# A hybrid decoder layer on one core: projections, S5 scan and attention heads in one written order, and the third modulation moved to the merge

## The chip, the core and the metric

The kernel runs on one core of a Trainium2 chip. The metric is the device time of one execution, in microseconds, as the median of several runs. The engines that matter are TensorE (PE, with its weight loads PEld), VectorE (DVE), ScalarE (ACT), GpSimd (POOL) and the DMA queue of SyncE (SPq). Each of them takes its own instructions in the order in which the program lists them, and waits where an input or a buffer isn't ready.

## The reference

One decoder layer for one sequence of 512 tokens and 2048 channels, in float32. A conditioning vector gives six modulations of 2048 values. The normed input is projected to queries, keys and values (8 heads of 128), a forget gate, an S5 input of 512 channels and two gates of 2048. S5 is a complex scan along the tokens (2048 states); the heads are causal softmax attention with a bias from the summed forget gate. Both results go through an up-projection, are weighed by their gates, added and projected by `w_out`. A feed-forward with 16384 retrieved experts follows.

```python
mod = cond @ w_ada[l] + b_ada[l]
sh1, sc1, g1, sh2, sc2, g2 = jnp.split(mod, N_MOD, axis=-1)
h = modulate(rms_norm(x, norm1_w[l]), sh1, sc1)
proj = h @ w_in[l]
q, k, v, f_logit, u, gate_s, gate_a = jnp.split(proj, IN_SPLIT_POINTS, axis=-1)
y_ssm = half_glu(s5_mixer(u, ...), w_glu[l], b_glu[l])
y_attn = fox_attention(q, k, v, f_logit, b_forget[l], q_norm_w[l], k_norm_w[l])
merged = (jax.nn.sigmoid(gate_s) * (y_ssm @ w_ssm_up[l])
          + jax.nn.sigmoid(gate_a) * (y_attn @ w_attn_up[l]))
x = x + g1[:, None, :] * (merged @ w_out[l])
...
```

## The kernel before

All weights are float32 and are multiplied in three passes: each is split into a rounded part `whi` and a rest `wlo`, and three matmuls (`L82` to `L84`, or `L147` to `L149`) make one product. A unit of weights is four blocks of 128 rows by 256 columns, 512 KB: `wload` fetches it into `wf`, ACT casts it to `whi` (`L88`), DVE subtracts to get `wlo` (`L89`), and 48 matmuls of 256 columns or 24 of 512 use it. `whi` and `wlo` have two buffers each.

The stages follow each other. **Start** computes the first two modulations, the normed input `h` and the S5 input `u`, and prepares S5's constants; the tables of cosines and sines (`ctab`, `stab`) are built on POOL there. **Projections** come next: the forget gate, then for each pair of heads `hp` the queries, keys and values (`proj_tok`, four units each), and at the end the first gates. `qk` norms queries or keys: raw copies out of PSUM (`L743`), eight squares with sums on DVE (`L748`), a root on ACT (`L190`), small steps on DVE (`L191` to `L195`), a multiplication (`L753`), eight transposes on PE (`L759`). S5 and the heads run beside the projections: `tick()` is called after each unit and lets the generators in `self.bg` take steps, S5 half a step and the heads one. An S5 step is a quarter of a 128-channel block: two products `bu` on PE, multiplications and scans on DVE, six multiplications and sums on POOL (`L692` to `L698`), and products into `y` on PE (`L700`, `L701`). A head's step scores one block of 128 tokens and transposes and multiplies the earlier ones (`L790` to `L815`). The third modulation, `ada(2, ...)`, is worked on there too: 64 tiles `adaw` of 256 KB, each multiplied into a sum on DVE (`L247`).

A scheduler sets the order within this stage: it puts instructions where their inputs are due, and the loads and splits of weights stand first (`high_priority(4000)`). Only the start and the experts are in written order (`manual_schedule`).

**Half GLU and merge** follow: eight rounds `jp`, each one unit of S5's up-projection, two of the heads', and eight of the next gates. `ada` for the last three modulations runs beside them, 12 calls of 16 tiles `y` of 256 KB. These take their buffers from the pool `yp` with 28 buffers, of which 24 hold the heads' and S5's results. Then come `w_out`, the routes to the experts, and the experts themselves.

Of the kernel before, what the change touches and what calls it, by code (L numbers as in the profile page):

```python
# [17 lines left out]
P = 128  # L18
S = 512
# [19 lines left out]
TODO = ('tg', '', 'tgw', '', 'tg', '', 'tg', 'm')  # L39
PE_ROWS = (2, 3, 5, 6, 7, 12)  # L40
# [17 lines left out]
class Builder:  # L58
# [77 lines left out]
    def proj_tok(self, w2d, nk, c0, act, pool, tag):  # L136

        mm = self.nc.tensor.matmul
        ps = [self.t(pool, [P, 2, 256], F32, tag) for _ in range(2)]
        for k0 in range(0, nk, 4):  # L140
            hi, lo = self.wunit(w2d, k0, 4, c0, 256)
            for t in range(TT):
                o = ps[t // 2][:, t % 2, :]
                for k in range(4):
                    kk = k0 + k
                    ah, al = (x[:, t * P:(t + 1) * P] for x in act(kk))
                    mm(o, ah, hi[:, k, :], start=kk == 0 and t % 2 == 0, stop=False, skip_group_check=True)  # L147
                    mm(o, ah, lo[:, k, :], start=False, stop=False, skip_group_check=True)
                    mm(o, al, hi[:, k, :], start=False, stop=kk == nk - 1, skip_group_check=True)  # L149
            self.tick()  # L150
        return ps
# [105 lines left out]
    def start(self, es, w_u):  # L257


        nc, V, G = self.nc, self.nc.vector, self.nc.gpsimd  # L260
# [19 lines left out]
        def load():  # L280

            while seq and (free or seq[0][0] == "x"):
# [18 lines left out]
                tiles[key] = t, slot  # L301

# [40 lines left out]
        def rest(q, accs, rows):  # L343
# [8 lines left out]
            ws = []  # L352
            for c in range(2):
                wf = take("w", q, c)
# [4 lines left out]
                load()  # L359
# [11 lines left out]
            late = None  # L371
            for k in range(q * 4, q * 4 + 4):
# [97 lines left out]
    def s5_setup(self, loads):  # L470
# [24 lines left out]
        cs, sn = nt("s5c0"), nt("s5s0")  # L495
# [22 lines left out]
        for l in range(7):  # L518
            c2, s2, tq = (self.t(cp if l == 6 else self.s5w, [P, J], F32, f"s5p{l}{x}") for x in "cst")
# [11 lines left out]

        ct = self.ct = self.t(self.tabp, [P, J, P], F32, "ctab")
        st = self.st = self.t(self.tabp, [P, J, P], F32, "stab")
        nc.gpsimd.memset(ct[:, :, 0:1], 1.0)
        nc.gpsimd.memset(st[:, :, 0:1], 0.0)
        n = 1
        for l in range(7):
            cb = pc[l][:, :, None].to_broadcast([P, J, n])
            sb = pn[l][:, :, None].to_broadcast([P, J, n])
            tm = self.t(self.s5w, [P, J, n], F32, "tabt")  # L540
            lo, hi = slice(0, n), slice(n, 2 * n)
# [74 lines left out]
    def s5_mats(self, m):  # L616
        nc, sp = self.nc, self.s5p
        bt = []
        for i in range(2):
            ps = self.t(self.ptp, [P, P], F32, "tp")  # L620
            nc.tensor.transpose(ps, self.pb[i][:, 4 * m:4 * m + 4].rearrange("p j a c -> p (j a c)"), self.ident)
            b = self.t(sp, [P, 4, P], F32, "bt", bufs=2)
            nc.gpsimd.memset(b, 0.0)
            for jj in range(4):
                r = slice(32 * jj, 32 * jj + 32)
                nc.scalar.copy(b[r, jj, :], ps[r, :])
            bt.append(b)
        ctm = []
        for i in range(2):
            ps = self.t(self.ptp, [P, P], F32, "tp")  # L630
            nc.tensor.transpose(ps, self.cd[i][:, m].rearrange("p a s -> p (a s)"), self.ident)
            c = self.t(sp, [P, 640], F32, "cm", bufs=2)
            nc.gpsimd.memset(c, 0.0)
            for g in range(2):
                r = slice(64 * g, 64 * g + 64)
                dst = c.rearrange("p (j r) -> p j r", r=160)[r, :, 16 * g:16 * g + 16]
                src = ps.rearrange("p (j r) -> p j r", r=32)[r, :, 16 * g:16 * g + 16]
                nc.scalar.activation(dst, src, AF.Copy, scale=1.0 if i == 0 else -1.0)
            ctm.append(c)
        return bt, ctm  # L640

    def s5_tile(self, m, jj, bt, u):
        nc, sp = self.nc, self.s5p
        j = 4 * m + jj
        br = self.t(self.ps5, [P, S], F32, "bu", bufs=2)
        nc.tensor.matmul(br, bt[0][:, jj, :], u, start=True, stop=True)
        bi = self.t(self.ps5, [P, S], F32, "bu", bufs=2)
        nc.tensor.matmul(bi, bt[1][:, jj, :], u, start=True, stop=True)
        c4 = self.ct[:, j, None, :].to_broadcast([P, 4, P])
        s4 = self.st[:, j, None, :].to_broadcast([P, 4, P])  # L650

        def v(x):
# [4 lines left out]
        wi = self.t(sp, [P, S], F32, "w", bufs=4)
        tm = self.t(sp, [P, S], F32, "tmv")
        V.tensor_mul(v(tm), v(bi), s4)
        V.tensor_mul(v(wr), v(br), c4)  # L660
        V.tensor_add(wr, wr, tm)
        tm = self.t(sp, [P, S], F32, "tmv")
        V.tensor_mul(v(tm), v(br), s4)
        V.tensor_mul(v(wi), v(bi), c4)
        V.tensor_sub(wi, wi, tm)
        mg = self.mag[:, j:j + 1].to_broadcast([P, P])
        rc, rs = self.rot[0][:, j:j + 1], self.rot[1][:, j:j + 1]
        ini = (0.0, 0.0)
        for c in range(4):
            sl = slice(c * P, (c + 1) * P)  # L670
            V.tensor_tensor_scan(wr[:, sl], mg, wr[:, sl], ini[0], op0=ALU.mult, op1=ALU.add)
            V.tensor_tensor_scan(wi[:, sl], mg, wi[:, sl], ini[1], op0=ALU.mult, op1=ALU.add)
            if c < 3:
                q = self.t(sp, [P, 4], F32, "car", bufs=4)
                e = slice(c * P + P - 1, c * P + P)
                V.tensor_mul(q[:, 0:1], wi[:, e], rs)
                V.tensor_mul(q[:, 1:2], wr[:, e], rs)
                V.scalar_tensor_tensor(q[:, 2:3], wr[:, e], rc, q[:, 0:1], op0=ALU.mult, op1=ALU.subtract)
                V.scalar_tensor_tensor(q[:, 3:4], wi[:, e], rc, q[:, 1:2], op0=ALU.mult, op1=ALU.add)
                ini = (q[:, 2:3], q[:, 3:4])  # L680
        return wr, wi, c4, s4

    def s5_out(self, jj, wr, wi, c4, s4, ctm, yps):
        nc, sp, G = self.nc, self.s5p, self.nc.gpsimd

        def v(x):
            return x.rearrange("p (c t) -> p c t", c=4)

        sr = self.t(sp, [P, S], F32, "s", bufs=2)
        si = self.t(sp, [P, S], F32, "s", bufs=2)  # L690
        tp = self.t(sp, [P, S], F32, "tmg")
        G.tensor_mul(v(tp), v(wi), s4)  # L692
        G.tensor_mul(v(sr), v(wr), c4)
        G.tensor_sub(sr, sr, tp)
        tp = self.t(sp, [P, S], F32, "tmg")
        G.tensor_mul(v(tp), v(wr), s4)
        G.tensor_mul(v(si), v(wi), c4)
        G.tensor_add(si, si, tp)  # L698
        cs = slice(jj * P, (jj + 1) * P)
        nc.tensor.matmul(yps, ctm[0][:, cs], sr, start=jj == 0, stop=False)  # L700
        nc.tensor.matmul(yps, ctm[1][:, cs], si, start=False, stop=jj == 3)  # L701

    def s5(self, m):
        nc = self.nc
        bt, ctm = self.s5_mats(m)
        yps = self.t(self.ps5, [P, S], F32, "y", bufs=1)
        u = self.u[m]
        z = None
        for jj in range(5):
            zn = self.s5_tile(m, jj, bt, u) if jj < 4 else None  # L710
            if z:
                self.s5_out(jj - 1, *z, ctm, yps)
            z = zn
            yield
        nc.vector.scalar_tensor_tensor(u, u, self.col2[:, 6 + m:7 + m], yps, op0=ALU.mult, op1=ALU.add)


    def forget(self, fps):
        nc, ap = self.nc, self.attp
        z = self.t(ap, [NH, S], F32, "fz")  # L720
# [1139 lines left out]
```

## Time and profile before

| | us |
|---|---|
| median of 3 runs | 3833.74 |
| lowest and highest | 3831.94, 3837.95 |
| the profiled execution, its time | 3826.62 |
| its span in the trace | 3824.6 |
| start, 0 to 173.8 | 173.8 |
| projections, S5, heads, half GLU, 173.8 to 744.1 | 570.3 |
| merge, 744.1 to 1209 | 464.9 |
| `w_out`, 1209 to 1396 | 187.0 |
| routes, 1396 to 1710 | 314.0 |
| experts, 1710 to the end | 2114 |

The limits of the stages are read from the trace, where the first or last instruction of a stage stands. The profiled execution is 7.1 us shorter than the median, and 2.0 us of its time lie outside its span. PE is busy for 3640.0 us of the span. A busy PE isn't always a PE at full speed: its granted clock is shown in each window, and matmuls overlap each other.

### The profile page before, as it was taken

Reading aid. Unit: us, or ns where it says so; the run is one execution under the profiler, and the core shown is the slowest. Engines: PE = TensorE matmul, PEld = TensorE weight load, DVE = VectorE, ACT = ScalarE, POOL = GpSimd, SP = SyncE. Lnnn points to the kernel's source line nnn. Section 1 sums busy time; section 2 is a strip of 40 time slices with the busy share of each in tenths; the row PEclk is TensorE's granted clock in tenths of the full one; section 3 lists DMA queues with packets and bytes.
Section 4 is the critical chain, followed back from the end, with each engine's and each line's share of the span. In section 5 each row is a group of like instructions: output and inputs, shape, how many; then the busy total and the mean of one; then the engine's idle time right before and its main releaser. Section 6 shows DMA issues by size and latency. Waiting matters only on the chain.

```text
span 3824.6 us, 58662 instructions
## 1 busy us (share of the span) xinstructions
PE 3640.0 (95%) x22966; PEld 3346.6 (88%) x22966; DVE 3027.7 (79%) x4704; ACT 1287.6 (34%) x2140; POOL 928.9 (24%) x680
## 2 busy tenths in 40 slices
PE   5988889999999999999989999999999999999998
PEld 2576768778887879899989999999999999999997
DVE  7678776555555358967879999999999988999997
ACT  2323323522222242245643333333333333333332
POOL 4142331000000024523411222222222212222221
PEclk8999989999999999999999999999999999999999
DMA  7723223366665542238889999999999979999996
GB/s 272 253 67 94 78 74 115 116 204 209 193 194 160 142 117 82 93 114 305 299 315 305 347 369 372 369 354 372 370 369 368 367 282 324 374 371 352 370 369 217
DMA packets 467081, 967.39 MB, mean 253 GB/s; under 512 B 66378, under 2 KB 335860, under 8 KB 400116
## 3 DMA queue, kind: packets, MB, share of 16 engines
q1 hardware_dynamic: 411508, 560.97, 44.9%
q0 software_dynamic: 55296, 402.68, 27.2%
q8 instruction: 180, 2.95, 0.3%
q14 instruction: 97, 0.79, 0.1%
HBM read 926.51 MB, written 36.96 MB: 252 GB/s over the span
## 4 chain that ended last, share of the span: by engine, by line
PE 78%; DVE 13%; DMA 4%; POOL 2%; issue 2%; ACT 1%; SPq 0%; DVEq 0%; ACTq 0%; POOLq 0%
PE A L84 8%; PE A L82 8%; PE A L83 8%; PE V L83 7%; PE V L84 7%; PE V L82 7%; PE tp L1426 6%; PE mm L82 4%; PE mm L84 4%; PE mm L83 4%; PE mx L82 2%; PE mx L83 2%; PE mx L84 2%; PE W L1262 2%; DMA y<-in_w_ada_dram 1%
## 5 line engine op out<-in xcount | busy, mean ns | idle before, releaser
L82 PE MATMUL V<-ghi,vhi 128*128 128x320 f32 x2048 | 651.8, 318 | 7.1 <-ACT vhi L1406 6.7
L82 PE MATMUL A<-hi,uhi 128*128 128x320 f32 x2048 | 657.6, 321 | 0.0
L84 PE MATMUL V<-ghi,vlo 128*128 128x320 f32 x2048 | 633.9, 310 | 3.9 <-DVE vlo L1409 3.9
L83 PE MATMUL V<-glo,vhi 128*128 128x320 f32 x2048 | 634.0, 310 | 1.6 <-DVE glo L1487 1.5
L84 PE MATMUL A<-hi,ulo 128*128 128x320 f32 x2048 | 633.0, 309 | 0.0
L83 PE MATMUL A<-lo,uhi 128*128 128x320 f32 x2048 | 632.6, 309 | 0.0
L1430 ACT CAST uhi<-tp 128x512 fp32r<-128x512 f32 x512 | 301.1, 588 | 609.5 <-PE tp L1426 608.3
L1336 DVE SCALAR_TENSOR_TENSOR big<-g,av,big 128x2048 f32<-128x2048 f32 x190 | 445.5, 2345 | 9.7 <-DMA g<-in_peer_v_dram,ids 7.2
L1324 DVE SCALAR_TENSOR_TENSOR g<-g,big 128x2048 f32<-128x2048 f32 x192 | 438.4, 2284 | 16.9 <-DMA g<-in_peer_u_dram,ids 8.0
L88 ACT CAST whi<-wf 128x1024 fp32r<-128x1024 f32 (+1 forms) x209 | 217.5, 1041 | 692.8 <-PE mx L83 223.9
L89 DVE TENSOR_TENSOR wlo<-wf,whi 128x1024 fp32r<-128x1024 f32 (+1 forms) x174 | 228.6, 1314 | 213.0 <-ACT whi L88 185.8
L82 PEld LDWEIGHTS V<-ghi,vhi 128*128 128x128 f32 x2048 | 385.9, 188 | 9.4 <-ACT vhi L1406 6.9
L84 PEld LDWEIGHTS V<-ghi,vlo 128*128 128x128 f32 x2048 | 385.3, 188 | 4.3 <-DVE vlo L1409 4.3
L83 PEld LDWEIGHTS V<-glo,vhi 128*128 128x128 f32 x2048 | 386.3, 189 | 2.7 <-DVE glo L1487 2.6
L83 PEld LDWEIGHTS A<-lo,uhi 128*128 128x128 f32 x2048 | 386.0, 188 | 0.0
L82 PEld LDWEIGHTS A<-hi,uhi 128*128 128x128 f32 x2048 | 385.7, 188 | 0.0
L84 PEld LDWEIGHTS A<-hi,ulo 128*128 128x128 f32 x2048 | 384.7, 188 | 0.0
L1437 DVE TENSOR_TENSOR ulo<-tp,uhi 128x512 fp32r<-128x512 f32 x428 | 291.1, 680 | 52.1 <-ACT uhi L1430 42.7
L1409 DVE TENSOR_TENSOR vlo<-vf,vhi 128x1024 fp32r<-128x1024 f32 x248 | 302.4, 1220 | 31.6 <-ACT vhi L1406 31.5
L1406 ACT CAST vhi<-vf 128x1024 fp32r<-128x1024 f32 x248 | 259.5, 1047 | 167.4 <-PE V L83 130.4
L1426 PE MATMUL tp<-ident,uf 128*128 128x128 f32 x2048 | 306.5, 272 | 0.3 <-DVE ulo L1437 0.3
L247 DVE SCALAR_TENSOR_TENSOR y<-y,cond,y 128x512 f32<-128x512 f32 x180 | 141.8, 788 | 172.8 <-DMA y<-in_w_ada_dram 171.4
(471 smaller groups left out, 7505.1 us busy)
## 6 DMA issues: line engine op xcount, KB each, us to landing
uf<-in_peer_u_dram SPq DMA_DIRECT2D x128, 1024.0 KB
vf<-in_peer_v_dram SPq DMA_DIRECT2D x248, 512.0 KB
wf<-in_w_in_dram SPq DMA_DIRECT2D x115, 512.0 KB
y<-in_w_ada_dram SPq DMA_DIRECT2D x192, 256.0 KB
wd<-ev SPq DMA_DIRECT2D x40, 512.0 KB
wt<-wd SPq DMA_DIRECT2D x128, 160.0 KB
adaw<-in_w_ada_dram SPq DMA_DIRECT2D x32, 512.0 KB
wf<-in_w_ada_dram SPq DMA_DIRECT2D x32, 512.0 KB
```

The source lines that it names most:

```text
L82: mm(ps, lhi, rhi, start=start, stop=False)
L83: mm(ps, lhi, rlo, start=False, stop=False)
L84: mm(ps, llo, rhi, start=False, stop=stop)
L88: nc.scalar.copy(hi, src)
L89: return (lo_eng or nc.vector).tensor_sub(lo, src, hi.bitcast(F32))
L1324: V.scalar_tensor_tensor(g, g, 1.0, hr, op0=ALU.mult, op1=ALU.mult, accum_out=av[:, s:s + 1])
L1336: V.scalar_tensor_tensor(acc, g, av[:, s:s + 1], acc, op0=ALU.mult, op1=ALU.add)
L1406: nc.scalar.copy(vhi, vf)
L1409: V.tensor_sub(vlo, vf, vhi.bitcast(F32))
L1426: mm(tp[:, k], ufs[i][:, (4 * c + k) * P:(4 * c + k + 1) * P], self.ident, is_transpose=True, start=k == 0, stop=False, skip_group_check=True)
L1430: nc.scalar.copy(hi, tp)
L1437: late.append(on_pe if i < ND0 - 3 else lambda: V.tensor_sub(lo, tp, hi.bitcast(F32)))
```

## The change

The forget gate, the queries, keys and values, and the first gates now take their units from one list, `stream(units)`, and stand with S5 and the heads in one `manual_schedule()`: what the program says is the order of every engine there. A unit is worked on in quarters of 12 matmuls (in the gates, too). After its first quarter the next unit's `whi` is cast; `tick()` follows each quarter; after the first `tick()` the next unit's `wlo` is made.

S5 is one generator with about ten steps for each of its 16 blocks. It builds its tables itself, on DVE (48 instructions), and its last six operations are on DVE as well. The squares in `qk` are on ACT. `qk` is a generator of 11 steps, and a head has 14, in the order "s0", "r0 s1", "r1 s2", "t0" and so on. The rates of steps for each `tick()` are 1.0 for `qk` and the forget gate, 0.66 for heads (1.0 during the first gates), and 2.0 for S5 until the first queries are done, 0.92 afterwards. `tick()` itself is as it was: it adds the rate to `b[2]` at each call, whether the list `b[0]` has a generator in it or not.

The lower parts of the weight splits in the start go from POOL to DVE. `ada(2, ...)` leaves the projections; the merge has two calls in each round, 16 calls and 256 tiles in all. The gates of round 1 stand ahead of the merge of round 0.

```diff
+RT = 2.0
+R5 = 0.92
+RH = 0.66
+RL = 1.0
...
+    def uhi(self, i):
+        if i < len(self.units):
+            cols = self.units[i][3]
+            hi, lo = (self.t(self.wpool, [P, 4, cols], F32R, x, bufs=2) for x in ("whi", "wlo"))
+            self.nc.scalar.copy(hi, self.uf[i])
+            self.us[i] = hi, lo
+
+    def ulo(self, i):
+        if i < len(self.units):
+            hi, lo = self.us[i]
+            self.nc.vector.tensor_sub(lo, self.uf.pop(i), hi.bitcast(F32))
+            self.uload()
+
+    def unit(self, parts):
...
+        hi, lo = self.us.pop(i)
+        for n, part in enumerate(parts):
+            part(hi, lo)
+            if n == 0:
+                self.uhi(i + 1)
+            self.tick()
+            if n == 0:
+                self.ulo(i + 1)
...
-                self.split(hi, lo, wf, G)
+                nc.scalar.copy(hi, wf)
...
+            for c, sub in enumerate(subs):
+                V.tensor_sub(*sub)
+                take("w", q, c)
+                load()
...
-            nc.gpsimd.tensor_mul(tm, st[:, :, lo], sb)
-            nc.gpsimd.tensor_mul(ct[:, :, hi], ct[:, :, lo], cb)
-            nc.gpsimd.tensor_sub(ct[:, :, hi], ct[:, :, hi], tm)
...
+    def s5(self):
+        nc, sp, V = self.nc, self.s5p, self.nc.vector
+        yield from self.s5_tables()
+        bt = [self.t(sp, [P, 4, P], F32, f"bt{i}") for i in range(2)]
+        cm = [self.t(sp, [P, 640], F32, f"cm{i}") for i in range(2)]
+        for x in bt + cm:
+            V.memset(x, 0.0)
+        yield
...
-        G.tensor_mul(v(tp), v(wi), s4)
-        G.tensor_mul(v(sr), v(wr), c4)
-        G.tensor_sub(sr, sr, tp)
...
+            V.tensor_mul(v(tm), v(wi), s4)
+            V.tensor_mul(v(sr), v(wr), c4)
+            yield
+            V.tensor_sub(sr, sr, tm)
...
-                    nc.vector.scalar_tensor_tensor(j, x[:, t, h], 1.0, x[:, t, h], op0=ALU.mult, op1=ALU.mult,
-                                                   accum_out=ms[:, 2 * b + t, h:h + 1])
+                    nc.scalar.activation(j, raw[b][:, t, h], AF.Square, accum_out=ms[:, 2 * b + t, h:h + 1])
...
-        for i in range(TT + 2):
-            if i < TT:
-                score(i)
-            if 0 <= i - 1 < TT:
-                trans(i - 1)
-            if 0 <= i - 2 < TT:
-                value(i - 2)
+        for step in ("s0", "r0 s1", "r1 s2", "t0", "r2 s3", "t1", "r3 v0", "t2", "v1", "t3", "v2", "v3"):
+            for x in step.split():
+                {"s": score, "r": scale, "t": trans, "v": value}[x[0]](int(x[1]))
             yield
...
+            bs5 = [[self.s5()], RT, 0.0]
+            bpo = [[], 1.0, 0.0]
+            bat = [[], RH, 0.0]
+            self.bg = [bpo, bat, bs5]
+            bpo[0].append(self.forget(self.mproj(1)[0]))
+            for hp in range(4):
+                qs, ks = [], []
+                bpo[0].append(self.qk(self.raw(self.mproj_tok()), self.col2[:, 0:1], qs))
+                bs5[1] = R5
+                bpo[0].append(self.qk(self.raw(self.mproj_tok()), self.col2[:, 1:2], ks))
+                v = self.v_tok(self.mproj_tok())
+                self.flush(bpo)
+                self.flush(bat)
+                bat[0].extend(self.head(hp * 2 + i, qs, ks, v) for i in range(2))
+            bat[1] = RL
+            sg = self.gates(0, self.apool, "a")
...
-            self.ada(2, hp, self.adap, 2)
...
+        sgs = [sg, self.gates(1, self.apool, "a")]
         for jp in range(8):
-            self.merge(jp, sg, ys, yh)
-            if jp < 7:
-                sg = self.gates(jp + 1, self.sgp, "sg")
-            for n in range(3 * jp // 2, 3 * (jp + 1) // 2):
-                self.ada(3 + n % 3, n // 3, self.yp, tag="y")
+            self.merge(jp, sgs.pop(0), ys, yh)
+            if 0 < jp < 7:
+                sgs.append(self.gates(jp + 1, self.sgp, "sg"))
+            for n in range(2 * jp, 2 * jp + 2):
+                self.ada(2 + n % 4, n // 4, self.yp, tag="y")
```

How the order of instructions moves is shown at three places. The names are tiles with the number that the program gives them; `x2` is two instructions of that form.

The first is on PE, around the transposes of a normed tile (`t`) in the first pair of heads. Before, they stand in the key phase (`mm_1719` and `mm_1720` are its accumulators):

```order
L149 MATMUL mm_1719<-whi_1777,h_821 128x256
L147 MATMUL mm_1720<-whi_1777,h_774 128x256
L148 MATMUL mm_1720<-wlo_1778,h_774 128x256
L759 MATMUL tp_1705<-ident_64,t_1676 128x128 x2
L759 MATMUL tp_1712<-ident_64,t_1676 128x128 x2
L149 MATMUL mm_1720<-whi_1777,h_775 128x256
...
L149 MATMUL mm_1720<-whi_1777,h_821 128x256
L759 MATMUL tp_1705<-ident_64,t_1686 128x128 x2
L759 MATMUL tp_1712<-ident_64,t_1686 128x128 x2
L147 MATMUL mm_1720<-whi_1777,h_774 128x256
```

After, in the phase that follows the one whose tile is normed (`mm_1705` is its accumulator):

```order
L201 MATMUL mm_1705<-whi_1616,h_547 128x256
L202 MATMUL mm_1705<-wlo_1617,h_547 128x256
L203 MATMUL mm_1705<-whi_1616,h_548 128x256
L867 MATMUL tp_1750<-ident_64,t_1701 128x128 x2
L867 MATMUL tp_1750<-ident_64,t_1703 128x128 x2
L867 MATMUL tp_1757<-ident_64,t_1701 128x128 x2
L867 MATMUL tp_1757<-ident_64,t_1703 128x128 x2
L201 MATMUL mm_1705<-whi_1616,h_501 128x256
```

What moved: the two halves `t` stood apart, with 11 projection matmuls between them; now all eight transposes stand together, behind the first 12 matmuls of the phase, and so they do for all eight normed tiles.

The second is on PE at the beginning of the first pair of heads. Before (`L779` is the head's bias, `L790` a score):

```order
L149 MATMUL mm_2438<-whi_2441,h_608 128x256
L779 MATMUL tp_2493<-fz_1325,PT_2494 128x512
L790 MATMUL tp_2501<-a_2072,a_1710 128x128
L147 MATMUL mm_2437<-whi_2671,h_774 128x256
L148 MATMUL mm_2437<-wlo_2672,h_774 128x256
...
L148 MATMUL mm_2437<-wlo_2672,h_789 128x256
L790 MATMUL tp_2511<-a_2072,a_1710 128x256
L149 MATMUL mm_2437<-whi_2671,h_790 128x256
```

After (`L889` the bias, `L901` scores, `L920` transposes, `L929` products with the values):

```order
L203 MATMUL mm_2398<-whi_2318,h_548 128x256
L889 MATMUL tp_2417<-fz_1337,oh_2415 128x512
L901 MATMUL tp_2423<-a_2094,a_1755 128x128
L901 MATMUL tp_2433<-a_2094,a_1755 128x256
L901 MATMUL tp_2443<-a_2094,a_1755 128x384
L920 MATMUL tp_2450<-ident_64,S_2425 128x128
L901 MATMUL tp_2457<-a_2094,a_1755 128x512
...
L929 MATMUL tp_2496<-PT_2489,a_2394 128x128 x2
L929 MATMUL tp_2496<-PT_2489,a_2396 128x128 x2
L889 MATMUL tp_2505<-fz_1337,oh_2503 128x512
L901 MATMUL tp_2511<-a_2101,a_1762 128x128
```

What moved: the head's matmuls stood between projection matmuls; now the whole head stands in one piece, and the second head of the pair (`tp_2505`) follows it in the same piece. There are four such pieces, one for each pair.

The third is on DVE in the merge. Before, between the `wlo` of successive units stand the sums of the modulations (`y`):

```order
L89 TENSOR_TENSOR wlo_7236<-wf_7233,whi_7235 128x1024
L247 SCALAR_TENSOR_TENSOR y_7412<-y_7455,cond_93,y_7412 128x512
L247 SCALAR_TENSOR_TENSOR y_7412<-y_7458,cond_93,y_7412 128x512
L89 TENSOR_TENSOR wlo_7266<-wf_7263,whi_7265 128x1024
L245 TENSOR_SCALAR y_7821<-y_7822,cond_93 128x512
L247 SCALAR_TENSOR_TENSOR y_7821<-y_7825,cond_93,y_7821 128x512
L89 TENSOR_TENSOR wlo_7296<-wf_7293,whi_7295 128x1024
L247 SCALAR_TENSOR_TENSOR y_7821<-y_7828,cond_93,y_7821 128x512
L89 TENSOR_TENSOR wlo_7326<-wf_7323,whi_7325 128x1024
```

After:

```order
L95 TENSOR_TENSOR wlo_6955<-wf_6952,whi_6954 128x1024
L301 SCALAR_TENSOR_TENSOR y_7172<-y_7197,cond_93,y_7172 128x512
L301 SCALAR_TENSOR_TENSOR y_7172<-y_7200,cond_93,y_7172 128x512
L301 SCALAR_TENSOR_TENSOR y_7172<-y_7203,cond_93,y_7172 128x512
L301 SCALAR_TENSOR_TENSOR y_7172<-y_7206,cond_93,y_7172 128x512
L95 TENSOR_TENSOR wlo_6985<-wf_6982,whi_6984 128x1024
L301 SCALAR_TENSOR_TENSOR y_7172<-y_7209,cond_93,y_7172 128x512
L301 SCALAR_TENSOR_TENSOR y_7172<-y_7212,cond_93,y_7172 128x512
L301 SCALAR_TENSOR_TENSOR y_7172<-y_7215,cond_93,y_7172 128x512
L95 TENSOR_TENSOR wlo_7015<-wf_7012,whi_7014 128x1024
```

What moved: where two or fewer sums stood between two `wlo`, there are now three or four.

## Rows read from the trace of the kernel before

**Rows 1.** Stage windows: us; then busy (count) PE, PEld, DVE, ACT, POOL; PEclk, DMA.

```profile
173.80:744.10 570.30, 499.46 (x3155) 424.99 (x3156) 396.79 (x891) 201.62 (x374) 152.23 (x108) 0.93 0.30 91
744.10:1209.00 464.90, 460.10 (x2015) 370.79 (x2014) 270.59 (x332) 110.60 (x127) 24.83 (x15) 1.00 0.65 199
```

**Rows 2.** Waits of 173.8 to 744.1: us in total, times, longest.

```profile
PE tp L759 <- DVE t L753: 29.8, 9, 7.0
...
PE tp L805 <- ACT S L798: 18.8, 8, 5.0
...
PE y L701 <- POOL s L698: 12.0, 5, 2.6
...
PE y L700 <- POOL s L694: 5.8, 3, 2.6
```

**Rows 3.** Timeline: start, duration; two successive projection matmuls of 256 columns, two of 512.

```profile
263.05 0.28 PE L148 MATMUL mm<-wlo,h 128*128 128x256 f32 x1
...
263.17 0.28 PE L149 MATMUL mm<-whi,h 128*128 128x256 f32 x1
...
685.03 0.39 PE L83 MATMUL mm<-h,whi 128*128 128x512 f32 x1
...
685.26 0.40 PE L84 MATMUL mm<-h,wlo 128*128 128x512 f32 x1
```

**Rows 4.** Timeline from 229.8: the end of a query norm beside POOL.

```profile
229.84 0.17 DVE L191 RECIPROCAL ms<-ms 128x8 f32<-128x8 f32 x1
...
230.97 1.29 POOL L693 TENSOR_TENSOR s<-w,ctab 128x512 f32<-128x512 f32 x1
...
231.06 1.22 DVE L193 TENSOR_TENSOR ms<-ms,ms 128x8 f32<-128x8 f32 x1
...
234.82 0.69 DVE L753 TENSOR_TENSOR t<-t,ms 128x512 f32<-128x512 f32 x1
```

**Rows 5.** Groups of 173.8 to 744.1: busy us, mean ns, idle before.

```profile
L89 DVE TENSOR_TENSOR wlo<-wf,whi 128x1024 fp32r<-128x1024 f32 x59 | 87.0, 1475 | 96.8 <-ACT whi L88 96.3 <-DMA adaw<-in_w_ada_dram 0.4
L88 ACT CAST whi<-wf 128x1024 fp32r<-128x1024 f32 x59 | 61.7, 1047 | 171.0 <-PE mm L149 122.7 <-issue 16.8 <-DVE car L677 16.5
...
L743 ACT COPY t<-mm 128x512 f32<-128x512 f32 x16 | 9.2, 577 | 8.9 <-PE mm L149 8.9
L190 ACT ACT_TABLE_LOAD x7 | 9.0, 1283 | 0.1
...
L665 DVE TENSOR_TENSOR w<-w,tmv 128x512 f32<-128x512 f32 x16 | 10.7, 667 | 0.0
```

**Rows 6.** Timeline of one head, 680.17 to 697.43.

```profile
680.17 1.12 PE L779 MATMUL tp<-fz,PT 8*128 8x512 f32 x2
...
684.00 0.40 ACT L796 ACTIVATE S<-S,sm 128x128 f32<-128x128 f32 x1 [0.78 <-DVE sm L795]
...
684.40 0.49 ACT L796 ACTIVATE S<-S,sm 128x256 f32<-128x256 f32 x1
...
693.85 0.72 ACT L798 ACTIVATE S<-S,sm 128x512 f32<-128x512 f32 x1 [0.23 <-DVE sm L797]
...
696.03 1.09 PE L814 MATMUL tp<-PT,a 128*128 128x128 f32 x8
...
697.16 0.27 ACT L815 COPY yo<-tp 128x128 f32<-128x128 f32 x1 [0.90 <-PE tp L814]
```

**Rows 7.** Merge: groups of DVE, busy us, mean ns, idle before.

```profile
L247 DVE SCALAR_TENSOR_TENSOR y<-y,cond,y 128x512 f32<-128x512 f32 x180 | 141.8, 788 | 172.8 <-DMA y<-in_w_ada_dram 171.4
L89 DVE TENSOR_TENSOR wlo<-wf,whi 128x1024 fp32r<-128x1024 f32 x80 | 100.8, 1260 | 6.5 <-ACT whi L88 6.2
```

**Rows 8.** Windows of 20 us in the merge, line L247 alone: DVE busy (count), PEclk, DMA.

```profile
760.00:780.00 20.00, 8.99 (x11) 1.00 0.71 226
...
980.00:1000.00 20.00, 3.76 (x5) 1.00 0.55 156
800.00:820.00 20.00, 6.76 (x9) 1.00 0.74 225
```

More of the change, by code (lines that the diff above doesn't have):

```diff
@@ L145, in proj_tok @@
                     kk = k0 + k
-                    ah, al = (x[:, t * P:(t + 1) * P] for x in act(kk))
+                    ah, al = (x[:, t * P:(t + 1) * P] for x in self.h[kk])
                     mm(o, ah, hi[:, k, :], start=kk == 0 and t % 2 == 0, stop=False, skip_group_check=True)
                     mm(o, ah, lo[:, k, :], start=False, stop=False, skip_group_check=True)
-                    mm(o, al, hi[:, k, :], start=False, stop=kk == nk - 1, skip_group_check=True)
-            self.tick()
+                    mm(o, al, hi[:, k, :], start=False, stop=kk == KT - 1, skip_group_check=True)
+            self.unit([lambda hi, lo, t=t: part(hi, lo, t) for t in range(TT)])
         return ps
@@ L301, in load @@
                 tiles[key] = t, slot
+            if not seq:
+                for slot in list(free):
+                    if slot[0] is self.wpool:
+                        free.remove(slot)
+                        self.uload()
         def take(*key):
@@ L614, in s5_setup @@
             self.cd.append(c)
[L616 to L640, printed above, removed]
@@ L657, in s5_tile @@
[L657 to L668, printed above, removed]
@@ L669, in s5_tile @@
[L669 to L680, printed above, removed]
@@ L703, in s5, with inputs @@
[L703 to L713, printed above, removed]
-            yield
-        nc.vector.scalar_tensor_tensor(u, u, self.col2[:, 6 + m:7 + m], yps, op0=ALU.mult, op1=ALU.add)
+        def inputs(m):
+            tps = []
+            for i in range(2):
+                ps = self.t(self.ptp, [P, P], F32, "tp")
+                nc.tensor.transpose(ps, self.pb[i][:, 4 * m:4 * m + 4].rearrange("p j a c -> p (j a c)"), self.ident)
+                for jj in range(4):
+                    r = slice(32 * jj, 32 * jj + 32)
+                    nc.scalar.copy(bt[i][r, jj, :], ps[r, :])
@@ new lines, in first, with last @@
+        def first(j):
+            m, jj = divmod(j, 4)
+            b = bus[j] = [self.t(self.ps5, [P, S], F32, "bu", bufs=2) for _ in range(2)]
+            for i in range(2):
+                nc.tensor.matmul(b[i], bt[i][:, jj, :], self.u[m], start=True, stop=True)
+        def last(j):
+            m, jj = divmod(j, 4)
+            if jj == 0:
+                self.yps = self.t(self.ps5, [P, S], F32, "y", bufs=1)
+            sr, si = ys.pop(j)
+            cs = slice(jj * P, (jj + 1) * P)
+            nc.tensor.matmul(self.yps, cm[0][:, cs], sr, start=jj == 0, stop=False)
+            nc.tensor.matmul(self.yps, cm[1][:, cs], si, start=False, stop=jj == 3)
@@ L718, in forget @@
+        last(NJ - 1)
+        yield
+        yield
+        end(3)
     def forget(self, fps):
         nc, ap = self.nc, self.attp
-        z = self.t(ap, [NH, S], F32, "fz")
+        z = self.cum = self.t(ap, [NH, S], F32, "fz")
         nc.vector.tensor_scalar(z, fps[0:NH, :], self.bf, None, op0=ALU.add)
@@ L725, in forget @@
         nc.scalar.activation(e, e, AF.Ln, bias=1.0)
+        for _ in range(6):
+            yield
         nc.vector.scalar_tensor_tensor(z, z, 0.0, e, op0=ALU.min, op1=ALU.subtract)
@@ L728, in forget @@
                                      op0=ALU.mult, op1=ALU.add)
-        self.cum = z
+        for _ in range(4):
+            yield
         ps = self.t(self.ptp, [P, TT, NH], F32, "tp")
@@ L1739, in build @@
         self.wa = a["w_ada"][0].rearrange("(p i) n -> p i n", i=KT)
-        with ExitStack() as r0, tc.manual_schedule():
-            self.start(r0, w[:, 3080:3592])
+        units = [(w, k, 3072, P) for k in range(0, KT, 4)]
+        for c in [x * 1024 + hp * 256 for hp in range(4) for x in range(3)] + list(GB):
+            units += [(w, k, c, 256) for k in range(0, KT, 4)]
+        self.stream(units)
         ppm = ctx.enter_context(ExitStack())
-        self.pmm = self.pool(ppm, "pmm", 3, PSUM)
```

293 lines of the change are left out of this document (189 added, 104 removed).

## The prediction

> **What bounds the kernel now.** I read the stage windows first, then the waits of the stage that is rewritten, then single places in the timeline. In the projection stage PE is busy for 499.5 of 570.3 us, and its clock averages 0.93; in the merge it is busy for 460.1 of 464.9 us at full clock [rows 1]. PE sets both. So a gain in the projection stage can only come from its 70.8 us of idle time and from its clock, and there is nothing to gain in the merge, only to lose.
>
> The waits say where the 70.8 us lie [rows 2]: 29.8 before the transposes of a normed tile (nine waits, the longest 7.0), 18.8 before the transposes of attention weights, 17.8 before S5's last products, where POOL was late (12.0 and 5.8). About 4 us are scattered. The clock is the second loss: an average of 0.93 over 570.3 us is 2 x 0.07 x 570 = 80 us at 1.2 instead of 2.4 GHz, which costs at most 40 us. Some of it falls on idle time; laying each matmul against its distance to the next, I put the loss at 30 us. The floor of the stage is then about 570 - 71 - 30 = 469 us.
>
> **What the change does, part by part.** I make the sum against the profiled execution, 3826.6 us, 7.1 below the median; the forecast adds the 7.1 back.
>
> *Credit.* The rates are meant to spread steps over quarters. But `tick()` adds the rate also while a list is empty, and the lists of norms and heads are empty for most of a phase. By the time a generator is appended, it has more credit than it has steps, and it runs to its end in the next tick. The order shows this: all eight transposes of a normed tile stand behind the first 12 matmuls of the next phase, and both heads of a pair stand in one piece without a projection matmul inside, four times. So the work that should cover the waits is not between the steps. I cost both from that.
>
> *Norms, eight.* When a phase ends, ACT copies the second raw tile (0.58), casts the next `whi` (1.05), and takes eight squares. No row shows a square with a sum; the nearest is an exponential of 128 columns with its sum, and the next one starts 0.40 later [rows 6], so 3.2 for eight. Then comes the root, with a table load of 1.28 in about half the cases [rows 5], five small DVE steps of 0.17 without POOL, and the multiplication of 0.69, twice [rows 4]. With hand-overs that is 7.4 us. In front of the transposes PE has 12 matmuls at a pitch of 0.12 [rows 3], 1.4 us. So PE waits 6.0 us, eight times: 48 in place of 29.8. Bounds: 3.3 each, the mean of the wait in the trace (29.8 over nine), and 7.0, its longest [rows 2]. I take 6.0 as it is nearer to the longest, which also had little in front of it.
>
> *Heads, eight.* The head at 680.17 lasts 17.3 us to the end of its last copy [rows 6], with projection matmuls and weight splits between its steps. About 3 us of that are steps waiting behind those, so alone it takes 14.3. Its own matmuls are 13 groups of 8.8 us together (the first and the last are in [rows 6]), less some 0.12 for each where a group's end overlaps the next: 7.3. PE then idles 7.0 us per head, 56 in place of 18.8. Bounds: 2.4 (18.8 over 8) and 10.0 (17.3 less 7.3).
>
> *S5 on DVE.* The six last operations of 16 blocks cost DVE 0.67 each [rows 5], 64 us; the 64 sums of `ada(2)` that leave (0.79 each in the merge [rows 7], 50 us) give most of that back. DVE is busy for 397 of 570 us [rows 1], so on average there is room, and the 17.8 us of waits for POOL go. But at the beginning there is none. At a rate of 2.0, 48 table instructions (18 of 512 columns at 0.67, the rest smaller: 19 us), four memsets and the `wlo` are queued on DVE in the time in which PE works through the forget gate and two units of queries, some 22 us; the queue is about 29 us long, and the first blocks then get five ticks each, about 11 us with S5's own products, for 13 us of DVE work. A `wlo` stands behind all that, and PE behind it. I take 14 us once; bounds 0 and 22. Scattered waits stay at 5.
>
> Idle is then 48 + 56 + 14 + 5 = 123 us, 52 more than now.
>
> *Clock.* In the trace, stretches at 1.2 GHz follow PE's longer waits. If the loss grew as the idle time, it would go from 30 to 52; if the waits bunch (a pair of heads is one long stretch), it stays. I take the middle, 41: plus 11; bounds 0 and plus 22.
>
> *Start.* The eight `wlo` leave POOL for DVE. They follow the modulations and precede the products of `u`; the stage is full of transfers, and a `wlo` takes 1.2 to 1.5 us on DVE [rows 5]. I take -3, bounds -5 and +5.
>
> *Third modulation.* Its own few matmuls, about 5 us on PE, leave the projections: -5. In the merge, 256 tiles instead of 192 pass through a pool with four free buffers, one or two of which hold a sum; so only two or three transfers are under way at once. DVE waits 172 us there for a tile [rows 7]. It is in order: a `wlo` behind a waiting sum waits, too, and PE behind it. Now 192 tiles go in 464.9 us, 2.42 each, at the pace of PE, and `wlo` itself waits only for ACT (6.2 us, [rows 7]), so the ring just keeps up. The change places three or four sums between two `wlo`, where two or three stood. 256 tiles at 2.9 to 3.0 per unit are spread over 87 units (80 of the merge, 7 of `w_out`), at 24 x 0.23 = 5.54 us [rows 3]: 482 us of PE. How fast can the ring go? The best window of 20 us has 11 tiles (1.82 each), others 9 (2.22), the slowest 5 [rows 8]. At 2.0 each the 256 need 512 us: plus 30. Bounds: 1.82 (466 us, hidden: 0) and 2.22 (568: plus 86).
>
> **Sum:** 52 + 11 - 3 - 5 + 30 = plus 85. 3826.6 + 85 + 7.1 = **3918 us**. With every bound at its low end the projection stage would gain; the order speaks against that.
>
> **The rivals.** *A, faster: without POOL the chains are short.* Mechanism: beside a POOL operation the same small DVE step takes 1.22 us that takes 0.17 otherwise, as if it waited for POOL's instruction to end [rows 4]. With POOL silent, the norm's chain may take 5.0 us and the head's 12.0. Idle: 8 x 3.6 + 8 x 4.7 + 0 + 5 = 72, plus 1; clock 25, minus 5; the start and `ada(2)`'s matmuls minus 10; a merge that hides everything 0. That gives 3826.6 - 14 + 7.1 = 3820, faster from the point at which norm and head together wait less than 10 us. For it: the step in [rows 4]. Against it: my chains have the short durations already, and PE's waits come from steps that follow each other, not from the length of each. The Trainium skill (SBUF — State Buffer, section "SBUF: two separate sides") says that DVE and GpSimd share a port pair that is locked for a whole instruction, and that a DVE operation with two SBUF inputs takes part in that lock against a GpSimd operation which reads SBUF. By that rule the change should help, and the trace agrees as far as the 1.22 against 0.17 us in [rows 4].
>
> *B, the ring sets the merge.* If more than two transfers are seldom under way, all 256 tiles keep today's mean of 2.42: 620 us in place of 482, plus 138. That gives 3918 + 108 = 4026. For it: 171 us of waits for tiles [rows 7]. Against it: the pace of today's mean is PE's, and 11 tiles in 20 us occur.
>
> *C, the merge hides all:* 3918 - 30 = 3888, inside the forecast's range.
>
> *D, it does what it says:* steps spread over quarters, waits of POOL gone, stage near its floor with 15 us of waits: 3826.6 - 71 + 15 - 20 + 7.1 = about 3758. The order excludes it unless the pieces are covered by something I don't see.
>
> **How the numbers follow.** Forecast with C: 0.70. A: 0.12. B: 0.08. D: 0.03. Between A and the forecast, within 0.2% (7.7 us, about what a measurement of this kernel can tell from no change): 0.07. So faster 0.15, same 0.07, slower 0.78. The range: the low end is 3830, between A and no change; the high end is 3985, the forecast with the merge's upper bound and some 10 us of the idle bounds. A, D and B lie outside, some 0.2.
>
> **What would show it.** Projection stage at about 628 us with PE idle for 120; eight waits of 4 to 7 us before the transposes behind the first 12 matmuls of a phase; four stretches of about 29 us in which PE is half idle, with no projection matmul; no waits of S5's last products; a stretch around 190 to 220 us in which PE waits for `wlo` while DVE is full. In the merge, `wlo` and then PE waiting for tiles, and a stage of about 490 to 500 us. The prediction is wrong if a pair of heads takes under 22 us, if the norm's waits are under 4 us, or if PE in the merge stays as busy as now; and if the second stage ends earlier than 570 us, rival A or D holds.

## The result and the profile after

| | before | after |
|---|---|---|
| median, us | 3835.72 (3831.94 to 3837.95, 4 runs) | 3894.56 (3887.62 to 3898.42, 4 runs) |
| the profiled execution, us | 3826.62 | 3898.42 |
| its span, us | 3824.6 | 3896.6 |

The changed kernel is slower: 1.0152 times the time before, with a 95% interval from 1.0135 to 1.017, or 58.8 us between the medians. The forecast was 3918 (3830 to 3985), so plus 85. The two profiled executions lie 71.8 us apart; 12.6 of these are in the routes and the experts, whose code is the same. The profile before happens to be short there (2428.4 us, against 2443.4 in that of `e4_ada` below, with the same code), so the stages ahead of them are compared.

Here are the stages of the kernel before once more, cut at the same instructions in both kernels (the last product of `u`, the last product of the half GLU, the last of the merge, the first sum of the second norm), and then those after. Columns: from and to, length, busy us and count of PE, PEld, DVE, ACT and POOL, the granted clock, the DMA share and GB/s.

```profile
0.00:172.80 172.80, 126.29 (x437) 59.99 (x437) 120.12 (x254) 52.70 (x77) 56.35 (x66) 0.89 0.78 266
172.80:744.50 571.70, 499.86 (x3157) 425.32 (x3158) 397.78 (x893) 202.97 (x377) 152.23 (x108) 0.93 0.30 91
744.50:1203.50 459.00, 457.77 (x2004) 369.02 (x2002) 265.20 (x325) 108.64 (x124) 23.19 (x14) 1.00 0.66 200
1203.50:1396.20 192.70, 188.44 (x816) 150.81 (x815) 74.02 (x87) 49.00 (x82) 6.18 (x3) 0.98 0.51 130
```

```profile
0.00:161.50 161.50, 130.41 (x437) 61.81 (x437) 98.19 (x260) 52.45 (x76) 2.25 (x12) 0.89 0.79 272
161.50:784.70 623.20, 529.22 (x3126) 444.14 (x3126) 368.19 (x846) 220.44 (x502) 0.00 (x0) 0.88 0.20 60
784.70:1257.60 472.90, 465.18 (x2033) 374.74 (x2033) 298.59 (x373) 108.87 (x125) 27.77 (x15) 1.00 0.70 218
1257.60:1455.60 198.00, 189.66 (x817) 150.62 (x815) 89.27 (x108) 49.60 (x81) 4.61 (x2) 0.98 0.59 155
```

Start minus 11.3, projections plus 51.5, merge plus 13.9, `w_out` plus 5.3: together plus 59.4, close to the 58.8 between the medians. In the projections PE's idle time grows from 71.8 to 94.0 us, and its busy time by 29.4 us with 31 matmuls fewer; the clock falls from 0.93 to 0.88. All this although DVE is less busy (368 against 398 us) and POOL does nothing.

The waits of PE in that stage after (us in total, times, the longest), against [rows 2]:

```profile
PE tp L867 <- DVE t L861: 44.9, 8, 7.4
PE tp L901 <- DVE S L903: 13.9, 8, 1.7
PE tp L920 <- ACT PT L922: 11.3, 9, 1.4
PE tp L920 <- ACT S L913: 8.1, 8, 1.1
PE tp L713 <- ACT bt L708: 4.9, 2, 4.3
PE tp L824 <- DVE fz L818: 4.1, 1, 4.1
PE tp L929 <- DVE S L903: 2.1, 5, 0.4
PE tp L901 <- ACT nc L891: 2.1, 8, 0.3
```

The waits for S5's last operations on POOL are gone. The eight waits of the norms are there, 5.6 us each. The waits of the heads (`L901`, `L920`, `L929`) are short and many, 37.5 us together, as steps without cover would be. How that looks at the beginning of a pair of heads, from the timeline (start, duration, the wait ahead in brackets):

```profile
299.28 1.12 PE L889 MATMUL tp<-fz,oh 8*128 8x512 f32 x2
...
300.44 0.59 ACT L891 COPY nc<-tp 128x512 f32<-128x512 f32 x1 [0.95 <-PE tp L889]
301.04 1.28 ACT L907 ACT_TABLE_LOAD   x1
301.06 0.35 DVE L903 SCALAR_TENSOR_TENSOR S<-tp,cq,nc 128x128 f32<-128x128 f32 x1 [4.90 <-ACT nc L891]
...
302.34 0.40 ACT L907 ACTIVATE S<-S,sm 128x128 f32<-128x128 f32 x1
...
302.86 0.16 DVE L912 RECIPROCAL sm<-sm 128x1 f32<-128x1 f32 x1 [0.81 <-ACT S L907]
...
303.56 0.30 PE L920 MATMUL tp<-ident,S 128*128 128x128 f32 x1 [1.14 <-ACT S L913]
```

Copy, table load, score, exponential, reciprocal and scale follow each other, while PE has only the next scores to do. The next projection matmul stands at 332.45; the four stretches without one last 33.1, 34.8, 32.8 and 32.5 us. In the first of them PE is busy for 23.8 us and idle for 9.4, at a mean clock of 0.70, which is about 20 us at 1.2 GHz (from and to, length, PE's busy us and count, clock, DMA):

```profile
299.28:332.45 33.17, 23.79 (x82) 0.70 0.02 9
```

### The profile page after: what moved, and what is told of

It reads as the page before. It is cut to its first block, busy times and chain, and to the rows that moved or that the text cites. A ratio compares the mean times of both kernels' runs of the same rounds, so it can differ in the third digit from the quotient of the medians.

```text
span 3896.6 us, 58629 instructions
## 1 busy us (share of the span) xinstructions
PE 3685.5 (95%) x22966; PEld 3375.0 (87%) x22966; DVE 3030.8 (78%) x4731; ACT 1305.8 (34%) x2265; POOL 725.8 (19%) x518
## 4 chain that ended last, share of the span: by engine, by line
PE 73%; DVE 12%; DMA 8%; ACT 3%; issue 2%; POOL 1%; SPq 0%; DVEq 0%; ACTq 0%; POOLq 0%
PE A L90 7%; PE A L88 7%; PE A L89 7%; PE V L90 7%; PE V L89 7%; PE V L88 7%; PE tp L1538 6%; DMA y<-in_w_ada_dram 5%; PE mm L201 2%; PE mm L203 2%; PE mm L202 2%; DVE y L301 2%; PE mm L88 2%; PE mm L90 2%; PE mm L89 2%
## 5 line engine op out<-in xcount | busy, mean ns | idle before, releaser
L94 ACT CAST whi<-wf 128x1024 fp32r<-128x1024 f32 x146 | 153.6, 1052 | 540.3 <-PE mx L89 217.4
L301 DVE SCALAR_TENSOR_TENSOR y<-y,cond,y 128x512 f32<-128x512 f32 x240 | 192.9, 804 | 148.4 <-DMA y<-in_w_ada_dram 145.3
L1538 PEld LDWEIGHTS tp<-ident,uf 128*128 128x128 f32 x2048 | 255.6, 141 | 15.5 <-issue 5.1
```

What stands on the lines that cost most here:

```text
L94: nc.scalar.copy(hi, src)
L301: nc.vector.scalar_tensor_tensor(acc, w, col, acc, op0=ALU.mult, op1=ALU.add)
L1538: mm(tp[:, k], ufs[i][:, (4 * c + k) * P:(4 * c + k + 1) * P], self.ident, is_transpose=True, start=k == 0, stop=False, skip_group_check=True)
```

## The experiments

**Credit only while there is something to spend it on.** The theory was that the bursts cost the time. `e1_spread` changes one line of the changed kernel:

```diff
         for b in self.bg:
-            b[2] += b[1]
+            if b[0]:
+                b[2] += b[1]
```

> The changed kernel, with one change in tick(): a rate is only added while its list has a generator in it, so that steps of norms and heads are spread over quarters. Theory (the bursts cost the time): the eight waits before the transposes of norms (45 us in the changed kernel) fall to some 10, the four stretches of a pair of heads without a projection matmul (133 us in sum, of which the heads' own matmuls need 58) go, and the clock loss falls with them; the projection stage shrinks from 622 us to about 510, the whole to about 3785. Rival (the stage is bound by DVE and by in-order queues once S5 is on DVE, wherever the steps stand): the waits move to the weight splits and the stage stays above 580, the whole above 3850.

Measured: 3745.84 us (3737.85 to 3754.78), a ratio of 0.9763 (0.9738 to 0.9787) to the kernel before. The projections of `e1_spread`, in the columns of above, and PE's longest waits there:

```profile
163.30:647.70 484.40, 469.30 (x3125) 405.21 (x3126) 362.93 (x846) 225.21 (x510) 0.00 (x0) 0.99 0.25 77
```

```profile
PE tp L714 <- ACT bt L709: 6.7, 2, 6.1
PE mm L88 <- issue: 4.0, 1, 4.0
PE y L734 <- DVE s L800: 0.9, 2, 0.7
PE tp L902 <- DVE S L904: 0.9, 1, 0.9
```

The stage is 139 us shorter than in the changed kernel, more than the theory said; its idle time falls from 94 to 15 us, no wait for a norm is left, and the clock rises to 0.99. The same instructions on the same engines, with the same rates (but for eight more table loads on ACT), are 3.8% faster when the steps stand apart. The rival, that DVE or the queues would hold the stage above 580 us, is out. With the steps spread, all parts of the change together are worth 2.4% against the kernel before; the bursts turn that into a loss. What the written order itself or the squares on ACT give was not tested apart.

**Norms alone, heads alone.** The condition of `e1_spread` for one of the two lists:

```diff
-            if b[0]:
+            if b[0] or b is not self.bg[0]:
```

> As e1_spread, but for the list of norms alone; heads keep their bursts. Theory: minus 35 us of waits and some 10 of clock: about 3850. Rival (waits move on to the next step): above 3885.

Measured: 3821.45 us (3815.37 to 3827.7), ratio 0.9962 (0.9947 to 0.9978); projections 551.4 us.

> As e1_spread, but for the list of heads alone; norms keep their bursts. Theory: minus 65 to 80 us: about 3820. Rival (heads in one piece are no dearer than heads between projections): above 3885. If the two are independent, the gains of e2_norms and e3_heads add up to that of e1_spread.

Measured (with `self.bg[1]`): 3834.48 us (3824.55 to 3840.91), ratio 0.9993 (0.998 to 1.0005); projections 566.4 us.

```profile
156.50:707.90 551.40, 504.65 (x3125) 424.88 (x3126) 365.56 (x846) 219.86 (x502) 0.00 (x0) 0.93 0.22 67
```

```profile
158.20:724.60 566.40, 492.85 (x3126) 423.89 (x3126) 364.75 (x846) 227.34 (x510) 0.00 (x0) 0.92 0.21 66
```

Against the changed kernel's 623.2, spreading the norms gives 72 us and spreading the heads 57; both together 139, about the sum of 129. Of the norms' 72 us 47 are idle time; the other 25 are PE's busy time, which falls with the same matmuls as the clock rises (0.88 to 0.93). Of the heads' 57 us only 20 are idle time and 36 busy time. In `e3_heads` the norms' waits, still in bursts, even grow from 44.9 to 55.1 us, which is the 10 us that the sum lacks:

```profile
PE tp L868 <- DVE t L862: 55.1, 8, 8.9
```

**The third modulation alone.** `e4_ada` is the kernel before with that one part of the change:

```diff
-            self.ada(2, hp, self.adap, 2)
...
-            for n in range(3 * jp // 2, 3 * (jp + 1) // 2):
-                self.ada(3 + n % 3, n // 3, self.yp, tag="y")
+            for n in range(2 * jp, 2 * jp + 2):
+                self.ada(2 + n % 4, n // 4, self.yp, tag="y")
```

> The kernel before, with one part of the change alone: the third modulation leaves the projections, and the merge has two calls in each round (256 tiles). Theory (the ring of tiles is a little too slow for 256): merge and the first part of the output projection plus 20 us, projections minus 5: about 3850. Rival 1 (the merge has room for them; what is longer in the changed kernel's merge comes from the order of the gates): 3825 to 3832. Rival 2 (DVE is freed in the projections, which gains more than the ring loses): under 3820.

Measured: 3825.06 us (3808.39 to 3829.09), ratio 0.9966 (0.9952 to 0.9979), so 0.3% faster, against the theory.

```profile
175.50:717.60 542.10, 495.04 (x3125) 422.13 (x3126) 348.18 (x831) 200.79 (x376) 147.08 (x108) 0.94 0.22 69
717.60:1183.10 465.50, 463.28 (x2034) 373.63 (x2033) 302.61 (x373) 108.89 (x125) 27.78 (x15) 1.00 0.69 222
1183.10:1382.20 199.10, 191.30 (x816) 152.37 (x814) 88.94 (x108) 49.52 (x81) 4.54 (x2) 0.97 0.58 154
```

```profile
PE tp L759 <- DVE t L753: 22.2, 10, 6.9
PE y L701 <- POOL s L698: 11.8, 5, 2.6
PE y L700 <- POOL s L694: 5.6, 3, 2.4
PE tp L805 <- ACT S L798: 4.3, 5, 1.6
```

Merge plus 6.5 and `w_out` plus 6.4 are in the direction of the theory, but smaller. The projections lose 29.6 us, not 5, and 24.8 of them are idle time: DVE has 50 us less of work, and the heads' waits fall from 18.8 to 4.3, the norms' from 29.8 to 22.2 [rows 2]. Sums on DVE lay in front of steps that PE waits for. One such place in the kernel before:

```profile
583.47 2.93 DVE L247 SCALAR_TENSOR_TENSOR acc<-adaw,cond,acc 128x512 f32<-128x512 f32 x2
...
586.32 0.21 DVE L797 RECIPROCAL sm<-sm 128x1 f32<-128x1 f32 x2
586.50 0.80 ACT L798 ACTIVATE S<-S,sm 128x128 f32<-128x128 f32 x2 [2.26 <-DVE sm L797]
...
586.96 0.33 PE L805 MATMUL tp<-ident,S 128*128 128x128 f32 x1 [2.26 <-ACT S L798]
```

The reciprocal stands behind two sums, which take 2.93 us together, and ACT and then PE wait 2.26 us for it. That the stage's transfers also became fewer (DMA 0.30 to 0.22) was not tested apart. Rival 2 has the mechanism, but the whole did not come under 3820, since merge and `w_out` cost 12.9 us. The time lies where rival 1 put it, without its reason: the merge had no room to take the tiles for nothing.

**More buffers for the tiles.** `e5_ring` is `e1_spread` with six free buffers for the merge's tiles in place of four:

```diff
-        self.yp = self.pool(r2, "yp", 28)
+        self.yp = self.pool(r2, "yp", 30)
```

> e1_spread with 30 instead of 28 buffers in the merge's pool, so that the modulation tiles have six free ones in place of four. Theory (the ring of tiles limits the merge a little): merge and output projection together shrink by 10 to 15 us towards those of the kernel before (652 us), the whole to about 3733. Rival (what is longer there is only PE's own work for 64 more sums, and waits that more buffers don't change): within 4 us of e1_spread.

Measured: 3733.91 us (3726.12 to 3742.95), ratio 0.972 (0.9698 to 0.9741). The first rows are merge and `w_out` of `e1_spread`, the second those of `e5_ring`:

```profile
647.70:1113.70 466.00, 463.55 (x2034) 373.78 (x2033) 301.06 (x373) 108.79 (x124) 27.69 (x15) 1.00 0.69 221
1113.70:1314.20 200.50, 191.30 (x816) 151.95 (x815) 89.25 (x108) 49.67 (x82) 4.64 (x3) 0.97 0.57 153
```

```profile
648.70:1111.10 462.40, 462.40 (x2035) 373.99 (x2034) 319.67 (x398) 109.35 (x126) 24.28 (x15) 1.00 0.73 237
1111.10:1297.70 186.60, 185.91 (x817) 148.97 (x815) 70.39 (x82) 48.53 (x82) 3.69 (x2) 1.00 0.51 130
```

17.5 us less in these two stages (12 between the medians), with PE busy from end to end in the merge. DVE's instructions show where they went: 25 more in the merge and 26 fewer in `w_out`. So the ring does limit the stream of tiles, and the price falls mostly in `w_out`. This is the fastest kernel of the study together with the last one.

**What GpSimd did.** Three kernels put one part of S5 or of the start back on GpSimd, in `e1_spread`. First the eight lower halves in the start:

```diff
-                V.tensor_sub(*sub)
+                nc.gpsimd.tensor_sub(*sub)
```

> e1_spread with the eight lower halves of the weight splits in the start on GpSimd again, where they were before; their place in the order stays. Theory (a lower half on GpSimd takes about twice as long as on DVE and the products of u wait for it): the start goes back from 163 to about 170 us or more. Rival (the 11 us in the start come from the tables' leaving GpSimd): the start stays within 3 us of 163.

Measured: 3753.65 us (3750.54 to 3758.09), ratio 0.9782 (0.9765 to 0.9799); the start 162.5 us, so the rival holds. But the profiles of the seven kernels with the start of `e1_spread` have it at 156.5 to 164.3 us; a cost of a few us couldn't be seen in one of them.

Then the tables, built in the start with the code of the kernel before:

```diff
-        self.powers = pc, pn
+        ct = self.ct = self.t(self.tabp, [P, J, P], F32, "ctab")
+        st = self.st = self.t(self.tabp, [P, J, P], F32, "stab")
...
+            nc.gpsimd.tensor_mul(ct[:, :, hi], ct[:, :, lo], cb)
...
-        yield from self.s5_tables()
```

> e1_spread with S5's tables built on GpSimd in the start again, as before the change. Theory (tables on DVE at the head of S5 cost PE a wait of about 8 us there, and their GpSimd work in the start slowed DVE): start plus 5 us, the waits at the head of the projections gone, minus 8: together about minus 3. Rival (the tables are what made the start longer): start back at 173, the whole plus 5 or more.

Measured: 3770.91 us (3760.98 to 3775.74), ratio 0.9827 (0.981 to 0.9845). The start of `e1_spread`, then start and projections of `e7_tab`:

```profile
0.00:163.30 163.30, 127.31 (x437) 59.40 (x437) 98.22 (x260) 52.58 (x77) 2.38 (x12) 0.92 0.78 269
```

```profile
0.00:171.30 171.30, 124.35 (x437) 57.68 (x437) 115.03 (x259) 52.45 (x77) 35.72 (x54) 0.90 0.75 257
171.30:663.60 492.30, 472.99 (x3125) 407.64 (x3126) 344.28 (x799) 225.40 (x510) 0.00 (x0) 0.98 0.25 76
```

With 33 us of tables on POOL the same DVE work in the start takes 115 instead of 98 us, and the start is 8 us longer. The three profiles with the tables on POOL (171.3, and 172.8 and 175.5 in the kernel before and `e4_ada`) all lie above the seven without, so the rival holds, and most of the 11.3 us which the change gained in the start is the tables'. The wait for `bt` is gone, as the theory said, but others came (the largest is 3.2, for a `wlo`): the projections are 8 us longer, with 19 us less on DVE, which was not expected. Why is open, as is the rest of the 25 us between the medians; the two profiled executions, the shortest of this kernel and the longest of `e1_spread`, lie only 6 apart.

Last, the six operations at the end of each S5 block:

```diff
-            V.tensor_mul(v(tm), v(wi), s4)
-            V.tensor_mul(v(sr), v(wr), c4)
+            nc.gpsimd.tensor_mul(v(tm), v(wi), s4)
+            nc.gpsimd.tensor_mul(v(sr), v(wr), c4)
```

> e1_spread with the last six operations of each S5 block on GpSimd again, all else as there. Rival A of the prediction (taking S5 off GpSimd is what shortens the chains, since DVE is held up while GpSimd works): projection stage plus 15 us or more, DVE's small steps at 1.2 us again. Theory (order, not the engine, makes the stage; DVE has room): within 6 us of e1_spread's 484 us for that stage.

Measured: 3762.38 us (3759.01 to 3764.97), ratio 0.98 (0.9783 to 0.9818).

```profile
162.90:656.00 493.10, 471.37 (x3125) 406.23 (x3126) 326.81 (x750) 225.12 (x510) 141.22 (x96) 0.98 0.25 75
```

The stage is 8.7 us longer: between the two expectations. PE now waits 5.2 us for the last operations on POOL (`y`, 4.1 and 1.1), against 0.9 for those on DVE in `e1_spread`. The same small DVE step of a norm (a product of two tiles of 128x8) in the kernel before and here (least, median and longest time of eight, in ns):

```profile
L193 DVE TENSOR_TENSOR ms<-ms,ms x8: 166/1185/1216, 231.1 to 654.2; 128x8 f32<-128x8 f32 x8
```

```profile
L857 DVE TENSOR_TENSOR ms<-ms,ms x8: 166/166/1196, 231.4 to 561.1; 128x8 f32<-128x8 f32 x8
```

And in `e1_spread`, with POOL silent:

```profile
L857 DVE TENSOR_TENSOR ms<-ms,ms x8: 166/167/169, 229.3 to 552.3; 128x8 f32<-128x8 f32 x8
```

So the hold-up beside POOL is real, but in this order most of these steps don't meet it, though POOL is busy for 141 us of the stage against 152 before.

**Zeros ahead of the tables.** `e9_zero` is `e5_ring` with S5's weight tiles cleared early, on GpSimd:

```diff
-        yield from self.s5_tables()
         bt = [self.t(sp, [P, 4, P], F32, f"bt{i}") for i in range(2)]
         cm = [self.t(sp, [P, 640], F32, f"cm{i}") for i in range(2)]
         for x in bt + cm:
-            V.memset(x, 0.0)
+            nc.gpsimd.memset(x, 0.0)
+        yield from self.s5_tables()
```

> e5_ring with the four tiles of S5's weights set to zero on GpSimd ahead of the tables, not on DVE behind them. Theory (PE's wait of 6 us at the head of the projections is for these, at the end of DVE's queue of table instructions): that wait goes to under 2 us, the whole to about 3728. Rival (the next thing in that queue, the first S5 products' multiplications and a wlo, holds PE for as long): within 2 us of e5_ring, 3734.

Measured: 3733.8 us (3723.27 to 3737.96), ratio 0.9734 (0.9712 to 0.9755). The wait of 6.1 us is gone, but 1.3 before the first products and 2.4 and 0.8 before the first `y` came in its place; the stage is 3.3 us shorter than in `e5_ring` (484.4 to 481.1) and the whole the same. The rival holds for the most part.

## Why the prediction was right, and where its sum was off

**Direction and mechanism.** The reading of the order was the step that decided, and it held: the list's credit makes bursts, and the bursts cost more than the change gains. In the projection stage the forecast and rival D, in which the steps are spread, are 134 us apart; the changed kernel and `e1_spread` are 139 apart. That D's 3758 us came so near to the 3746 of `e1_spread` is in part luck: the stage is 484 us where D has 494, the start 9.5 shorter, and merge and `w_out` 14.8 longer, which D left out.

The sum was 26 us too high, in us against the kernel before:

| | forecast | measured |
|---|---|---|
| idle time: norms | 48 | 44.9 |
| idle time: heads | 56 | 37.5 |
| idle time: S5's beginning | 14 | 9.0 |
| idle time: scattered | 5 | 2.6 |
| idle time, change | +52 | +22 |
| loss by the clock, change | +11 | +27 |
| rest of the stage (forecast: the third modulation's matmuls) | -5 | +2 |
| projection stage, change | +58 | +51.5 |
| start, change | -3 | -11.3 |
| merge and `w_out`, change | +30 | +19.2 |
| all, change | +85 | +59.4 |

**Norms.** Forecast 6.0 us each, measured 5.6. The parts listed for the chain add up to 7.7 us, not 7.4, without the root; at this size it makes no difference.

**Heads and clock.** The loss by the clock is counted as half of PE's busy time in the stretches at 1.2 GHz: 30 us before and 57 after, so plus 27, beyond the forecast's bound of 22. The failed step is that a pair's stretch was counted as idle time plus matmuls at full speed, 14.0 and 14.6 us. In the first stretch PE is idle for 9.4 us and busy for 23.8: the clock is at 1.2 GHz for some 20 of 33 us, so the heads' own matmuls take longer and fill the gaps. Less is idle and more goes to the clock; the two experiments apart say the same, with 36 of the heads' 57 us in busy time. That the stage is only 6.5 us off is luck in part, since idle time was 30 too high and the clock 16 too low.

**S5's beginning.** Forecast 14, measured 4.9 for `bt` and 4.1 for the forget gate, within the bounds. The wait for a `wlo` that was to show it is 0.7 us long in all.

**Third modulation, projections.** Forecast minus 5, as DVE seemed to have room on average; `e4_ada` shows minus 29.6 in the kernel before. An average of 397 of 570 us didn't say whether a sum lay in front of a step PE waits for. How much of the 29.6 the changed kernel itself got can't be read, since its bursts have other waits.

**Third modulation, merge.** Forecast plus 30, measured plus 19.2, within the bounds of 0 and 86. Of these only 10.6 are idle time of PE; 8.6 are its busy time, with 29 matmuls more in the merge. The forecast took the third modulation's matmuls out of the projections and put nothing for them here. Counted by the sums on DVE, 231 tiles have gone until the merge ends, 2.05 us each, where the forecast had 2.0 and the kernel before 2.44. The mechanism, few buffers for the tiles, is shown by `e5_ring`. Where it bites was only half foreseen: DVE's waits for tiles fall from 171 to 145 us although there are more tiles, and PE doesn't wait for `wlo` but for the sums themselves and, in `w_out`, for a step of the second norm behind the last tiles (784 to 1320 us):

```profile
DVE y L301 <- DMA y<-in_w_ada_dram: 145.3, 95, 3.6
...
PE tp L304 <- DVE y L301: 10.6, 8, 2.6
...
PE tp L1046 <- DVE a L1023: 4.5, 1, 4.5
```

Merge and `w_out` are 6.3 us longer here than in `e4_ada` (670.9 against 664.6). Whether that is the new place of the gates was not tested.

**Start.** Forecast minus 3 with bounds of 5, measured minus 11.3. The step looked at the eight lower halves, for which `e6_lo` shows no cost; `e7_tab` says that the tables' leaving POOL, which the forecast put at nothing in the start, is worth about 8. There rival A's mechanism did act: DVE's busy time fell from 120 to 98 us. The seven starts that spread over 8 us bound how exactly such a term can be read.

**Rivals.** A was wrong for the stage as changed, where the waits come from steps in a row. Where they are spread, taking S5's end off GpSimd is worth 9 us of the stage (`e8_tail`). By the rule of the Trainium skill that was weighed there (SBUF — State Buffer, "SBUF: two separate sides"), a DVE operation with two SBUF inputs and a GpSimd operation that reads SBUF exclude each other for a whole instruction; the trace agrees, with 1185 ns in the median beside POOL's S5 work and at most 169 ns without it. B didn't come: the tiles went faster than before.

## What to carry to other kernels

When background work is stepped by credit, count credit only while there is work to spend it on, and look at the order of instructions, not at the rates: the same code was 1.5% slower or 2.4% faster than the kernel before by that one condition. PE's waits cost more than their own length, as the matmuls that follow run at the lower clock: 72 us for 47 of idle time in the norms, 57 for 20 in the heads. A queue with room on average can still be what is late: ask what lies in front of the step that is waited for.

## What the runs showed of the hardware

A gap's cost in clock was larger than expected: spreading the eight norms took away 45 us of their waits and gave 72. In the first stretch of a pair of heads, with PE busy for 23.8 of 33 us but in short pieces, the clock was at 1.2 GHz for about 20 us. And work on POOL cost time on DVE: 33 us of it in the start made DVE's work there 17 us longer.
